# A woven inverse tail, spectra and tables stored as two parts, and pairwise sums, in a one-core hybrid encoder layer

## The chip, the cores and the metric

The kernel runs on one core of one Trainium2 chip. The metric is the device time of one execution in microseconds (us), lower is better. The core has a matrix engine (PE, with its weight loads listed apart as PEld), a vector engine (DVE), a scalar engine (ACT), GpSimd (POOL) and a queue that issues transfers (SP). Each takes its instructions in a fixed order, and all ordinary transfers of this kernel are issued by SP from one queue.

## The reference

One encoder layer on x of 4096 tokens by 1024, all float32. The inputs include the two filter MLPs' weights, convolution weights and gate matrices, which are left out here.

```python
xn = rmsnorm(x, norm_g)
proj = xn @ w_in                                 # 1024 -> 4608 columns: six groups of 768
v, x0, x1 = dwconv3(proj[:, 0:2304])             # centred, width 3
u = v * x1
k = two_sided_filter(MLP(positions)) * exp_window        # 2L points, L1-normalised per channel
y_hy = x0 * (irfft(rfft(u, 2L) * rfft(k, 2L))[:L] + hy_skip * u)
xb = dwconv4(proj[:, 3072:3840])
y_lru = scan_forward(xb) + scan_backward(xb)     # gated linear recurrences, 12 heads of 64
y = concat(rmsnorm(y_hy) * silu(gate_hy), rmsnorm(y_lru) * silu(gate_lru)) @ w_out
out = rmsnorm(x + y, final_g)
```

## The kernel before

Every matmul of float32 operands is done as three products. An operand is split into a high part, rounded to the matmul type, and a low part, the rest; high by high, high by low and low by high are summed in PSUM. A helper `split` (L499 to L501) makes the two parts: ACT copies, DVE subtracts. `mm3` (L503 to L506) issues the three products for 768 columns as six matmuls of 384 columns, so all transforms of the convolution share L506.

- **phase_x** (L238 to L261) normalises x, 128 tokens at a time: two half-row squares on ACT with a running sum, a square root, a reciprocal, transposes, and it stores each chunk of 512 tokens as two parts in DRAM (`xs`) for the later passes.
- **inproj** (L296 on) is the projection. It has 36 column blocks by 8 chunks, each a "unit" of 24 matmuls of 128x512 on L311 to L313. Blocks go in five passes of 7 or 8; `load_w` (L273 to L279) brings a block's weights in two halves of 256 KB (L277), which DVE splits (L278, L279). The first pass is made while x is normalised.
- **phase_filter** makes the filter and its first transform, 64 slices `j`: result `kw` (one part, 384 KB) goes to the table `efd`. **phase_u** does the same for u with 32 slices of 768 KB to `eud`; DVE casts and subtracts on L635 and L636.
- **phase_mid** (L653 on) goes over 64 frequencies `k`. It loads `ef` and `eu` (384 KB each, L658), splits them (ACT L659, POOL L660), loads a table (128 KB, L665) and splits it on POOL (L669, L670), makes two transforms of 6 matmuls, multiplies them as complex numbers (ACT L683 to L685, DVE L689 to L692), splits the product into `rs`, transforms back with 6 matmuls, and stores 384 KB to `eyd` (L703).
- **phase_iy** is the last transform: 32 units, each loading 768 KB of `eyd` (L736, three buffers by `NE`), splitting it (ACT L738, DVE L739), 12 matmuls of 384 columns (L745), one copy (L749) and two stores to `ytd` (L751).
- **phase_out** takes 256 tokens at a time in 32 tasks, one for each branch `r` (0 the convolution, 1 the recurrence). `prepare` loads S (the gate) and y, multiplies and splits them into `A`, squares y (L791), sums the six blocks on DVE with one strided reduction (L796), splits the sum on POOL (L798, L799) and sums over partitions on PE (L803), which gives the scale `rr`. `project` does 72 matmuls (L817 to L819) and adds to the output with `rr` (L821); `finish` normalises and stores. Tasks of r=1 run `LEAD` = 3 chunks ahead of those of r=0, which need `ytd`.

The order is set in two steps. `weave` merges the streams of the phases as they are written, by weights per step; then a scheduler with its own model of the engines fixes one order for each engine and for SP. The recurrence runs beside projection units, then the chain of phase_u, phase_mid and phase_iy beside the remaining 112 units, and phase_out comes last, alone. On SP at most 8 transfers are outstanding: each waits for the one eight before it. A store waits at the queue's head until its data are there, and everything behind it waits too.

Of the kernel before, what the change touches and what calls it, by code (L numbers as in the profile page):

```python
# [25 lines left out]
TC = 512  # L26
NE = 3
NO = 8
# [22 lines left out]
def shape_constants():  # L51
# [54 lines left out]
    fi = fi.reshape(2, 64, 64).transpose(1, 0, 2).reshape(128, 64)  # L106
    return dict(c_zf=zf, c_tn=tn, c_absd=absd.astype(f), c_fa=fa.astype(f), c_tabs=np.stack([tb, ib], 2).astype(f), c_fi=fi.astype(f))


@with_exitstack  # L110
def tile_hymba_block(ctx: ExitStack, tc: tile.TileContext, a: dict, out: bass.AP, dbg=None):
# [119 lines left out]
    def phase_x():  # L231
        tiles = []
        with tc.tile_pool(name="xp", bufs=1, side="right") as xp:
            for n in range(NCH):
# [3 lines left out]
                for q in range(4):  # L238
                    t0 = n * TC + q * P
                    nc.sync.dma_start(xt[q], a["x"][0, t0:t0 + P, :])  # L240
                    for h in range(2):
                        sq = xpool.tile([P, 4, P], F32, name="s4", bufs=3).rearrange("p k e -> p (k e)")
                        nc.scalar.activation(sq, xt[q][:, h * TC:(h + 1) * TC], AF.Square, accum_out=ss[:, h, q:q + 1])
                    qs = slice(q, q + 1) if n == 0 else slice(0, 4)
                    if n == 0 or q == 3:
                        nc.vector.tensor_tensor(rt[:, qs], ss[:, 0, qs], ss[:, 1, qs], ALU.add)
                        nc.scalar.activation(rt[:, qs], rt[:, qs], AF.Sqrt, bias=epsb, scale=1.0 / D)
# [270 lines left out]
    def phase_filter():  # L518
        with ExitStack() as st:
# [51 lines left out]
            hv3 = [t.rearrange("k (p j) -> k p j", j=64) for t in hid]  # L571
            ev = ef_d.rearrange("k r j c -> (k r) j c")
            def first_dft(j, kw, kr):
# [6 lines left out]
            for j in list(range(1, 64)) + [0]:  # L580
                lh = lhs[j % 2]
                for i in range(2):
# [11 lines left out]
                if pend is not None:  # L594
                    first_dft(*pend)
                kw = fw.tile([P, C], F32, name="kw", bufs=3)
                nc.vector.tensor_tensor(cv2(kw), hv(ps), cv2(win), ALU.mult)
# [16 lines left out]
                split(kr, kw)  # L614
                pend = (j, kw, kr)
                yield 0.8
# [3 lines left out]
    def phase_u():  # L620
        JB = 2
        with tc.tile_pool(name="uu", bufs=1) as up:
# [5 lines left out]
            nc.vector.tensor_tensor(fu[:, 1], f0, fu[:, 0].bitcast(F32), ALU.subtract)  # L628
            ev = eu_d.rearrange("k r j c -> (k r) j c")
            uv = ut_d.rearrange("(p j) c -> p j c", j=64)  # L630
            for g in range(64 // JB):
                ui = up.tile([64, JB, C], F32, name="uin", bufs=3)
                nc.sync.dma_start(ui, uv[:, g * JB:(g + 1) * JB, :])
                t = up.tile([P, JB, C], F32R, name="ut", bufs=2)
                nc.vector.tensor_copy(t[0:64], ui)  # L635
                nc.vector.tensor_tensor(t[64:], ui, t[0:64].bitcast(F32), ALU.subtract)  # L636
                stg = up.tile([P, JB, C], F32, name="ustg", bufs=3)
                for j in range(JB):
                    ps = aux_ps()
                    for h in range(2):  # L640
                        for w in range(2):
                            nc.tensor.matmul(ps[:, h, :NH], lhsT=fu[:, w], rhs=t[:, j, h * NH:(h + 1) * NH],  # L642
                                             start=w == 0, stop=w == 1)
                    nc.scalar.activation(cv2(stg[:, j]), hv(ps), AF.Copy)
                nc.sync.dma_start(ev[:, g * JB:(g + 1) * JB, :], stg)
                yield WU
# [6 lines left out]
    def phase_mid():  # L653
        with tc.tile_pool(name="mid", bufs=1) as mp:
            def load(src, s, name, eng):
                t = mp.tile([P, 2, C], F32R, name=name, bufs=3)
                raw = t[:, 1].bitcast(F32)
                nc.sync.dma_start(raw, src[s].rearrange("r j c -> (r j) c"))  # L658
                nc.scalar.activation(t[:, 0], raw, AF.Copy)  # L659
                eng.tensor_tensor(t[:, 1], raw, t[:, 0].bitcast(F32), ALU.subtract)  # L660
                return t

            def tabs(k):
                raw = mp.tile([P, 2, P], F32, name="traw", bufs=2)
                nc.sync.dma_start(raw, a["c_tabs"][:, k])  # L665
                r = []
                for i, (nm, nb) in enumerate((("tb", 2), ("ib", 2))):
                    t = mp.tile([P, 2, P], F32R, name=nm, bufs=nb)
                    nc.gpsimd.tensor_scalar(t[:, 0], raw[:, i], 1.0, 0.0, op0=ALU.mult, op1=ALU.add)  # L669
                    nc.gpsimd.tensor_tensor(t[:, 1], raw[:, i], t[:, 0].bitcast(F32), ALU.subtract)  # L670
                    r.append(t)
                return r

# [32 lines left out]
            for k in range(64):  # L706
                ef, eu = load(ef_d, k, "ef", nc.gpsimd), load(eu_d, k, "eu", nc.gpsimd)
                terms = []
# [45 lines left out]

    def phase_out():
        T = 256
        NM = L // T
        with tc.tile_pool(name="oa", bufs=1) as oa, tc.tile_pool(name="ob", bufs=1, side="right") as ob:
            identr = ob.tile([P, P], F32R, name="identr")
# [6 lines left out]
            def prepare(m, r):  # L766
# [13 lines left out]
                if r == 0:  # L780
                    for q in range(2):
                        yt = ob.tile([P, C], F32R, name="yt", bufs=2)
                        nc.sync.dma_start(yt.bitcast(F32), yt_d[m * T + q * P:m * T + (q + 1) * P, :])
# [14 lines left out]
                nc.gpsimd.tensor_copy(sr[:, 0], sy)  # L798
                nc.gpsimd.tensor_tensor(sr[:, 1], sy, sr[:, 0].bitcast(F32), ALU.subtract)  # L799
                pss = mm_ps()[:, 0:4].rearrange("p (q w) -> p q w", w=2)  # L800
# [5 lines left out]
                nc.vector.reciprocal(rr, rr)  # L806
                return A, rr

            def project(m, r, A, rr):
                for q in range(2):  # L810
                    ps = aux_ps()
                    for h in range(2):
                        sl = slice(h * 512, (h + 1) * 512)
                        for b in range(CB):
# [3 lines left out]
                            nc.tensor.matmul(ps[:, h], lhsT=ht, rhs=w[:, 1, sl], start=False, stop=False)  # L818
                            nc.tensor.matmul(ps[:, h], lhsT=lt, rhs=w[:, 0, sl], start=False, stop=b == CB - 1)  # L819
                    o = os_[m][q]  # L820
                    nc.vector.scalar_tensor_tensor(o, ps.rearrange("p h c -> p (h c)"), rr[:, q:q + 1], o,  # L821
                                                   op0=ALU.mult, op1=ALU.add)

            def finish(m):
                for q, o in enumerate(os_.pop(m)):
                    sq = ob.tile([P, D], F32, name="osq", bufs=2)
                    fs = ob.tile([P, 1], F32, name="fs", bufs=4)
# [10 lines left out]
            for i, t in enumerate(tasks):  # L838
                nxt = prepare(*tasks[i + 1]) if i + 1 < len(tasks) else None
                if i == 0:  # L840
                    for j in range(CB):
                        load_wo(j, main.tile([P, 2, KT, P], F32R, name="w", bufs=NW) if len(wos) < NW
                                else ob.tile([P, 2, KT, P], F32R, name=f"w{j}"),
                                lambda: oa.tile([P, TC], F32, name="ostg", bufs=2))
                    gfin.append(ob.tile([P, D], F32, name="gfin"))
                    nc.sync.dma_start(gfin[0], a["final_g"].partition_broadcast(P))
# [36 lines left out]
    phase_out()  # L883
    psctx.close()
# [29 lines left out]
```

## Time and profile before

| | us |
|---|---|
| median of 3 runs | 2957.67 (2956.57 to 2961.78) |
| the profiled execution | 2955.19 |
| its span in the trace | 2953.4 |
| PE busy in the span | 2848.1 (96%) |
| DVE, ACT, POOL busy | 1997.9, 1697.9, 705.9 |
| bytes moved | 699 MB, mean 237 GB/s |

The page's times are of the one profiled execution; the 1.8 us outside its span are its start and end. A busy PE is not a PE at its peak pace: matmuls overlap, so the time lost is read from gaps and from distances between starts. The span in 40 slices shows the PE at nine tenths or more nearly throughout, with dips in the first slice and around 2350 us, and the granted clock below full in two slices there.

### The profile page before, as it was taken

How to read it: one execution, taken by the hardware profiler on the slowest of the kernel's cores; microseconds unless marked ns; L12 is line 12 of the kernel's file. 1: busy time of each engine (PE TensorE's matmuls, PEld its weight loads, DVE VectorE, ACT ScalarE, POOL GpSimd, SP SyncE). 2: the span in 40 equal slices, each digit the busy share in tenths (PEclk: the TensorE clock that was granted, in tenths of full speed). 3: DMA queues.
4: the chain of work that ended last, by engine and by line, in shares of the span. 5: the costliest groups of instructions: out<-in, count | busy, mean ns of one | idle time of the engine just before them, and what ended most of it. 6: DMA issues, size and time to landing. Idle time of an engine off the chain costs nothing.

```text
span 2953.4 us, 37821 instructions
## 1 busy us (share of the span) xinstructions
PE 2848.1 (96%) x13211; PEld 2386.2 (81%) x13211; DVE 1997.9 (68%) x2144; ACT 1697.9 (57%) x2534; POOL 705.9 (24%) x910
## 2 busy tenths in 40 slices
PE   7999999999999999999999998999999799999998
PEld 6778888888887787877888887888888678888886
DVE  6998879664768856787664788666643366666665
ACT  4678887767787676764445675666645432222222
POOL 0013323210101201111004776766710010000001
PEclk9999999999999999999999999999999889999999
DMA  7566657437879877787997677666679865455542
GB/s 273 210 219 235 232 215 250 177 136 244 292 273 309 291 277 249 258 310 225 357 342 277 227 239 259 230 231 238 235 276 309 280 211 164 164 182 169 176 154 75
DMA packets 338238, 699.33 MB, mean 237 GB/s; under 512 B 33821, under 2 KB 156145, under 8 KB 337791
## 3 DMA queue, kind: packets, MB, share of 16 engines
q1 hardware_dynamic: 337918, 696.85, 67.9%
q8 instruction: 105, 1.72, 0.2%
q14 instruction: 87, 0.70, 0.1%
q0 software_dynamic: 128, 0.05, 0.0%
HBM read 445.13 MB, written 251.66 MB: 236 GB/s over the span
## 4 chain that ended last, share of the span: by engine, by line
PE 65%; DVE 13%; DMA 9%; issue 5%; ACT 5%; POOL 3%; SPq 1%; DVEq 0%; ACTq 0%; POOLq 0%
PE mm L311 12%; PE mm L312 12%; PE mm L313 12%; PE aux L506 8%; PE aux L819 4%; PE aux L817 4%; PE aux L818 4%; PE aux L443 3%; DVE cv L343 2%; PE aux L745 2%; DMA eu<-eud 2%; DMA x<-xs 2%; DVE sy L796 2%; PE aux L642 2%; DVE bb L470 1%
## 5 line engine op out<-in xcount | busy, mean ns | idle before, releaser
L311 PE MATMUL mm<-x,w 128*128 128x512 f32 x2304 | 909.3, 396 | 12.6 <-ACT cv L341 5.6
L312 PE MATMUL mm<-x,w 128*128 128x512 f32 x2304 | 907.6, 394 | 0.1
L313 PE MATMUL mm<-x,w 128*128 128x512 f32 x2304 | 905.2, 394 | 0.0
L311 PEld LDWEIGHTS mm<-x,w 128*128 128x128 f32 x2304 | 435.2, 189 | 105.3 <-DMA x<-xs 9.3
L313 PEld LDWEIGHTS mm<-x,w 128*128 128x128 f32 x2304 | 434.7, 189 | 84.4 <-issue 0.5
L312 PEld LDWEIGHTS mm<-x,w 128*128 128x128 f32 x2304 | 434.9, 189 | 84.1 <-issue 1.4
L817 PE MATMUL aux<-w,A 128*128 128x512 f32 x768 | 305.7, 398 | 19.0 <-DMA y<-yld 19.0
L343 DVE SCALAR_TENSOR_TENSOR cv<-raw,cols,cv 128x512 f32<-128x512 f32 (+2 forms) x336 | 260.7, 780 | 85.7 <-ACT cv L341 81.2
L819 PE MATMUL aux<-w,A 128*128 128x512 f32 x768 | 305.2, 401 | 0.0
L818 PE MATMUL aux<-w,A 128*128 128x512 f32 x768 | 304.4, 396 | 0.0
L798 POOL CAST sr<-sy 128x256 fp32r<-128x256 f32 x32 | 39.2, 1226 | 703.4 <-DVE sy L796 498.2
L660 POOL TENSOR_TENSOR ef<-ef 128x768 fp32r<-128x768 f32 x64 | 129.1, 2017 | 239.3 <-DMA eu<-eud 195.2
L817 PEld LDWEIGHTS aux<-w,A 128*128 128x128 f32 x768 | 146.1, 190 | 49.6 <-ACT A L793 19.3
L818 PEld LDWEIGHTS aux<-w,A 128*128 128x128 f32 x768 | 146.0, 190 | 32.0
L819 PEld LDWEIGHTS aux<-w,A 128*128 128x128 f32 x768 | 145.9, 190 | 30.9
L501 DVE TENSOR_TENSOR rs<-r,rs 128x768 fp32r<-128x768 f32 x65 | 94.1, 1447 | 108.3 <-ACT rs L500 108.3
L791 ACT ACTIVATE y<-y 128x1536 f32<-128x1536 f32 x32 | 47.7, 1490 | 202.8 <-DVE S L790 180.9
L333 ACT ACTIVATE raw<-mm 128x512 f32<-128x512 f32 x192 | 113.3, 590 | 86.0 <-PE mm L313 85.6
L443 PE MATMUL aux<-hl,wg 128*128 128x512 f32 x576 | 147.8, 392 | 5.4 <-ACT bb L445 5.2
L477 POOL TENSOR_TENSOR xb<-xb,bb 128x1024 f32<-128x1024 f32 x24 | 65.2, 2719 | 292.5 <-DVE bb L470 203.6
L660 POOL TENSOR_TENSOR eu<-eu 128x768 fp32r<-128x768 f32 x64 | 124.3, 1943 | 39.0 <-ACT eu L659 38.9
L443 PEld LDWEIGHTS aux<-hl,wg 128*128 128x128 f32 x576 | 107.3, 188 | 29.3 <-ACT bb L445 6.8
(201 smaller groups left out, 5023.6 us busy)
## 6 DMA issues: line engine op xcount, KB each, us to landing
x<-xs SPq DMA_DIRECT2D x256, 512.0 KB
hl<-hld SPq DMA_DIRECT2D x96, 512.0 KB
xs<-x SPq DMA_DIRECT2D x64, 512.0 KB
efd<-kw SPq DMA_DIRECT2D x64, 384.0 KB
sd<-cv SPq DMA_DIRECT2D x96, 256.0 KB
xb<-xbd SPq DMA_DIRECT2D x48, 512.0 KB
eud<-ustg SPq DMA_DIRECT2D x32, 768.0 KB
ef<-efd SPq DMA_DIRECT2D x64, 384.0 KB
```

The costliest lines, as they stand in the source:

```text
L311: nc.tensor.matmul(ps, lhsT=w[:, 0, kt, :], rhs=x[kt][:, 0], start=kt == 0, stop=False)
L312: nc.tensor.matmul(ps, lhsT=w[:, 0, kt, :], rhs=x[kt][:, 1], start=False, stop=False)
L313: nc.tensor.matmul(ps, lhsT=w[:, 1, kt, :], rhs=x[kt][:, 0], start=False, stop=kt == KT - 1)
L333: nc.scalar.activation(R[:, K - 1:K - 1 + TC], ps, AF.Copy)
L343: nc.vector.scalar_tensor_tensor(y[:, :N], R[:, k:k + N], w[k], y[:, :N], op0=ALU.mult, op1=ALU.add)
L443: nc.tensor.matmul(ps[:, h], lhsT=wg[:, u, gi, :], rhs=hl[h][:, v], start=k == 0, stop=k == 2)
L501: nc.vector.tensor_tensor(dst[:, 1], src, dst[:, 0].bitcast(F32), ALU.subtract)
L506: nc.tensor.matmul(ps[:, h, :NH], lhsT=lhs[:, x], rhs=rhs[:, y, h * NH:(h + 1) * NH], start=first and i == 0, stop=last and i == 2)
L660: eng.tensor_tensor(t[:, 1], raw, t[:, 0].bitcast(F32), ALU.subtract)
L817: nc.tensor.matmul(ps[:, h], lhsT=ht, rhs=w[:, 0, sl], start=b == 0, stop=False)
L818: nc.tensor.matmul(ps[:, h], lhsT=ht, rhs=w[:, 1, sl], start=False, stop=False)
L819: nc.tensor.matmul(ps[:, h], lhsT=lt, rhs=w[:, 0, sl], start=False, stop=b == CB - 1)
```

## The change

- Two-part storage. `efd` and `eud` hold a high and a low part, written by phase_filter (DVE subtracts the low part on a new line) and phase_u, so phase_mid loads 768 KB instead of 384 KB for each of `ef` and `eu` and splits neither. The transform table comes from the host as two parts; 65 transfers of 256 KB copy it from the input to a DRAM tensor `tabd` (written in phase_filter's loop), and phase_mid loads 256 KB per `k` from there. POOL does nothing in phase_mid any more.
- Buffers. `e` of phase_iy goes from 3 to 2, the staging of phase_u and of the filter (`kw`) from 3 to 2; phase_mid's table has 3.
- phase_u's cast moves from DVE to ACT.
- Weaving. 24 of phase_iy's 32 units are merged with phase_u, phase_mid and the projection; the last 8 (`TAIL`) come between phase_out's first tasks, which are of r=1. Pools of phase_out that need room come later (`late`).
- Sums. The strided reduction L796 becomes three elementwise adds; POOL's split becomes an ACT copy and a DVE subtract; the partition sums (`token_scale`) are made within `project`, after its first 36 matmuls.
- Squares. For the first chunk each whole row of 1024 is squared with a running sum once, by ACT for two of its tiles and by DVE for the other two.

```diff
-NE = 3
+NE = 2
+TAIL = 8
...
-    ef_d = dram.tile([64, 2, 64, C], F32, name="efd")
-    eu_d = dram.tile([64, 2, 64, C], F32, name="eud")
+    ef_d = dram.tile([64, 2, 64, 2, C], F32, name="efd")
+    eu_d = dram.tile([64, 2, 64, 2, C], F32, name="eud")
+    tab_d = dram.tile([P, 65, 2, 2, P], F32, name="tabd")
...
+                    if n == 0:
+                        sq = aux_ps().rearrange("p h c -> p (h c)")
+                        if q % 2:
+                            nc.vector.tensor_tensor_reduce(out=sq, in0=xt[q], in1=xt[q], scale=1.0, scalar=0.0, op0=ALU.mult,
+                                                           op1=ALU.add, accum_out=ss[:, 0, q:q + 1])
+                        else:
+                            nc.scalar.activation(sq, xt[q], AF.Square, accum_out=ss[:, 0, q:q + 1])
...
-                nc.scalar.activation(cv2(kw), hv(ps), AF.Copy)
-                nc.sync.dma_start(ev[:, j, :], kw)
+                nc.scalar.activation(cv2(kr[:, 0]), hv(ps), AF.Copy)
+                nc.vector.tensor_tensor(cv2(kr[:, 1]), hv(ps), cv2(kr[:, 0].bitcast(F32)), ALU.subtract)
+                nc.sync.dma_start(ev[:, j], kr.bitcast(F32))
...
             for j in list(range(1, 64)) + [0]:
+                nc.sync.dma_start(tab_d[:, j], a["c_tabs"][:, j])
...
-                raw = t[:, 1].bitcast(F32)
-                nc.sync.dma_start(raw, src[s].rearrange("r j c -> (r j) c"))
-                nc.scalar.activation(t[:, 0], raw, AF.Copy)
-                eng.tensor_tensor(t[:, 1], raw, t[:, 0].bitcast(F32), ALU.subtract)
+                nc.sync.dma_start(t.bitcast(F32), src[s].rearrange("r j w c -> (r j) w c"))
...
+                t = mp.tile([P, 2, 2, P], F32R, name="tab", bufs=3)
+                nc.sync.dma_start(t.bitcast(F32), tab_d[:, k])
+                return t[:, 0], t[:, 1]
...
-                sy = ob.tile([P, T], F32, name="sy", bufs=2)
-                nc.vector.tensor_reduce(sy, y.rearrange("p b t -> p t b"), axis=mybir.AxisListType.X, op=ALU.add)
+                nc.vector.tensor_tensor(y[:, 0:3], y[:, 0:3], y[:, 3:6], ALU.add)
+                nc.vector.tensor_tensor(y[:, 0], y[:, 0], y[:, 1], ALU.add)
+                sy = y[:, 0]
+                nc.vector.tensor_tensor(sy, sy, y[:, 2], ALU.add)
...
-                nxt = prepare(*tasks[i + 1]) if i + 1 < len(tasks) else None
+                nxt = prepare(*tasks[i + 1]) if i + 1 < len(tasks) and i + 1 != LEAD else None
+                if i < LEAD - 1:
+                    for _ in itertools.islice(tail, TAIL // (LEAD - 1)):
+                        pass
...
-    weave((proj, 144 - X2), (itertools.chain(phase_u(), phase_mid(), phase_iy()), (32 * WU + 129 * WM + 32 * WI) * S3))
+    last = phase_iy()
+    weave((proj, 144 - X2), (itertools.chain(phase_u(), phase_mid(), itertools.islice(last, 32 - TAIL)),
+                             (32 * WU + 129 * WM + (32 - TAIL) * WI) * S3))
```

The three places below show what the scheduler made of it. First, SP's queue at the start, where the weights of the first pass are loaded (`s` from `in_w_in`), before:

```order
12 L277 DMA s_339<-in_w_in_dram 128x4x128
13 L277 DMA s_343<-in_w_in_dram 128x4x128
14 L261 DMA xs_0_60<-x 128x1024
15 L261 DMA xs_1_61<-x 128x1024
16 L277 DMA s_348<-in_w_in_dram 128x4x128
17 L261 DMA xs_2_62<-x 128x1024
18 L277 DMA s_352<-in_w_in_dram 128x4x128
```

And the same place after, with the table copies (`tabd` from `in_c_tabs`, x8 being eight in a row):

```order
14 L596 DMA tabd<-in_c_tabs_dram 128x512 x2
15 L291 DMA s_337<-in_w_in_dram 128x4x128
16 L596 DMA tabd<-in_c_tabs_dram 128x512 x8
17 L291 DMA s_341<-in_w_in_dram 128x4x128
18 L596 DMA tabd<-in_c_tabs_dram 128x512 x3
19 L291 DMA s_346<-in_w_in_dram 128x4x128
20 L596 DMA tabd<-in_c_tabs_dram 128x512 x6
21 L291 DMA s_350<-in_w_in_dram 128x4x128
22 L596 DMA tabd<-in_c_tabs_dram 128x512 x3
```

All 65 copies stand in SP's rows 14 to 57, between the weight loads of the first pass, although they are written in the filter's loop; four of the sixteen weight halves stand behind all of them.

Second, PE's order where phase_mid's last inverse transform (`aux` from `rs`) stands, before; `mm` from `x,w` is a matmul of the projection:

```order
7155 L506 MATMUL aux<-rs,ib 128x384
7156 L313 MATMUL mm<-x,w 128x512
7157 L311 MATMUL mm<-x,w 128x512
7158 L312 MATMUL mm<-x,w 128x512
7159 L313 MATMUL mm<-x,w 128x512
7160 L506 MATMUL aux<-rs,ib 128x384 x5
7161 L311 MATMUL mm<-x,w 128x512
```

And after, where the last projection matmul (row 7534) stands:

```order
7531 L520 MATMUL aux<-rs,tab 128x384 x5
7532 L325 MATMUL mm<-x,w 128x512
7533 L326 MATMUL mm<-x,w 128x512
7534 L327 MATMUL mm<-x,w 128x512
7535 L520 MATMUL aux<-ef,tab 128x384 x6
7536 L520 MATMUL aux<-eu,tab 128x384 x6
7537 L520 MATMUL aux<-rs,tab 128x384 x6
7538 L520 MATMUL aux<-ef,tab 128x384 x6
```

Before, 426 projection matmuls follow the last inverse transform of phase_mid. After, none is left when 22 of its 65 `ef` transforms, 22 of `eu` and 23 of `rs` are still to come: PE has nothing else to do between them.

Third, PE's order where phase_out begins (`aux` from `w,A`), before:

```order
7649 L311 MATMUL mm<-x,w 128x512
7650 L312 MATMUL mm<-x,w 128x512
7651 L313 MATMUL mm<-x,w 128x512
7652 L745 MATMUL aux<-es,fi 128x384 x60
7653 L817 MATMUL aux<-w,A 128x512
7654 L818 MATMUL aux<-w,A 128x512
7655 L817 MATMUL aux<-w,A 128x512
```

And after:

```order
7600 L520 MATMUL aux<-rs,tab 128x384 x17
7601 L821 MATMUL mm<-onesr,sr 128x2 x8
7602 L755 MATMUL aux<-es,fi 128x384 x325
7603 L836 MATMUL aux<-w,A 128x512
7604 L837 MATMUL aux<-w,A 128x512
7605 L838 MATMUL aux<-w,A 128x512
```

Before, 5 units of phase_iy (60 matmuls) stand alone between the projection and phase_out. After, 27 of them (325 matmuls) stand alone, and the other 5 between 91 matmuls of phase_out's first task.

## Rows read from the trace of the kernel before

**Rows 1.** Windows: busy us (instructions) of PE, PEld, DVE, ACT, POOL; clock, DMA share, GB/s.
```profile
0.00:100.00 100.00, 85.23 (x370) 65.32 (x371) 75.46 (x156) 55.61 (x129) 3.06 (x11) 1.00 0.76 269
...
1400.00:1500.00 100.00, 97.13 (x448) 84.53 (x449) 65.11 (x54) 41.60 (x69) 0.00 (x0) 0.97 1.00 352
...
1700.00:1800.00 100.00, 93.24 (x437) 78.37 (x435) 83.59 (x85) 65.66 (x91) 73.66 (x66) 1.00 0.67 227
...
2300.00:2400.00 100.00, 76.59 (x353) 65.19 (x352) 47.95 (x38) 42.09 (x46) 9.38 (x6) 0.88 0.82 272
```

**Rows 2.** Shorter windows, the same columns.
```profile
30.00:40.00 10.00, 9.03 (x40) 7.16 (x39) 6.82 (x12) 4.70 (x12) 0.00 (x0) 1.00 1.03 369
...
60.00:70.00 10.00, 7.88 (x42) 6.20 (x41) 6.42 (x12) 4.38 (x13) 0.00 (x0) 1.00 0.08 32
1000.00:1005.00 5.00, 5.00 (x24) 4.13 (x22) 4.96 (x5) 4.39 (x5) 2.53 (x1) 1.00 1.03 419
...
2350.00:2360.00 10.00, 0.00 (x0) 0.00 (x0) 1.76 (x1) 0.40 (x1) 0.00 (x0) 0.50 1.04 374
```

**Rows 3.** Timeline of SP at the start: start us, us, engine, line.
```profile
51.36 0.38 SPq L277 DMA_DIRECT2D s<-in_w_in_dram  x1
```

**Rows 4.** Timeline of DVE at the start, the same columns.
```profile
54.52 0.43 DVE L278 CAST w<-s 128x512 fp32r<-128x512 f32 x1 [0.33 <-DMA s<-in_w_in_dram]
```

**Rows 5.** DMA issues: queue, count, KB each.
```profile
ef<-efd SPq DMA_DIRECT2D x64, 384.0 KB
...
eyd<-r SPq DMA_DIRECT2D x64, 384.0 KB
e<-eyd SPq DMA_DIRECT2D x32, 768.0 KB
...
s<-in_w_in_dram SPq DMA_DIRECT2D x72, 256.0 KB
...
traw<-in_c_tabs_dram SPq DMA_DIRECT2D x65, 128.0 KB
```

**Rows 6.** Timeline of PE: starts of two matmuls of 512 columns in phase_out.
```profile
2387.15 0.39 PE L818 MATMUL aux<-w,A 128*128 128x512 f32 x1
2387.38 0.39 PE L819 MATMUL aux<-w,A 128*128 128x512 f32 x1
```

**Rows 7.** Groups by shape, 1600 to 2150 us: busy, mean ns of one, idle before.
```profile
L692 DVE SCALAR_TENSOR_TENSOR r<-us,sgn,r 128x768 f32<-128x768 f32 x61 | 92.0, 1508 | 1.9
L501 DVE TENSOR_TENSOR rs<-r,rs 128x768 fp32r<-128x768 f32 x61 | 89.7, 1471 | 104.5 <-ACT rs L500 104.5
L506 PE MATMUL aux<-rs,ib 128*128 128x384 f32 x367 | 86.4, 346 | 20.7 <-DVE rs L501 11.0 <-issue 5.6 <-POOL tb L669 1.9
...
L691 DVE TENSOR_TENSOR r<-aux,ha 128x768 f32<-128x768 f32 x61 | 58.4, 958 | 1.7
```

**Rows 8.** Groups by shape, 300 to 600 us (the filter).
```profile
L501 DVE TENSOR_TENSOR kr<-kw,kr 128x768 fp32r<-128x768 f32 x45 | 42.9, 954 | 0.0
```

**Rows 9.** Groups by shape, 2050 to 2340 us (phase_iy).
```profile
L739 DVE TENSOR_TENSOR es<-e,es 128x1536 fp32r<-128x1536 f32 x32 | 56.3, 1759 | 88.2 <-ACT es L738 81.7 <-DMA x<-xs 6.5
L738 ACT ACTIVATE es<-e 128x1536 fp32r<-128x1536 f32 x32 | 47.4, 1482 | 8.3 <-DMA e<-eyd 5.1 <-DMA fz<-in_c_fi_dram 3.2
```

**Rows 10.** Timeline of PE where phase_out begins.
```profile
2335.07 2.35 PE L745 MATMUL aux<-es,fi 128*128 128x384 f32 x12 [1.35 <-DVE es L739]
2337.81 2.36 PE L745 MATMUL aux<-es,fi 128*128 128x384 f32 x12 [0.39 <-DVE es L739]
2341.32 2.19 PE L745 MATMUL aux<-es,fi 128*128 128x384 f32 x11 [1.15 <-DVE es L739]
2362.51 0.80 PE L817 MATMUL aux<-w,A 128*128 128x512 f32 x1 [19.01 <-DMA y<-yld]
```

**Rows 11.** Waits of PE: engine, line, for what, us in total, times, longest.
```profile
PE mm L803 <- POOL sr L798: 10.1, 16, 2.6
```

**Rows 12.** Groups by shape, 2340 us to the end (phase_out).
```profile
L796 DVE TENSOR_REDUCE sy<-y 128x256 f32<-128x1536 f32 x32 | 92.8, 2936 | 8.1 <-ACT y L791 8.1
```

More of the change, by code (lines that the diff above doesn't have):

```diff
@@ L240, in phase_x @@
                     nc.sync.dma_start(xt[q], a["x"][0, t0:t0 + P, :])
-                    for h in range(2):
+                    if n == 0:
[5 more added lines that the diff above has]
+                            nc.scalar.activation(sq, xt[q], AF.Square, accum_out=ss[:, 0, q:q + 1])
+                    for h in range(2 if n else 0):
                         sq = xpool.tile([P, 4, P], F32, name="s4", bufs=3).rearrange("p k e -> p (k e)")
@@ L706, in phase_mid @@
             for k in range(64):
-                ef, eu = load(ef_d, k, "ef", nc.gpsimd), load(eu_d, k, "eu", nc.gpsimd)
+                ef, eu = load(ef_d, k, "ef"), load(eu_d, k, "eu")
                 terms = []
@@ L752, in phase_iy, with phase_out @@
                 yield WI
-    def phase_out():
+    def phase_out(tail):
         T = 256
         NM = L // T
-        with tc.tile_pool(name="oa", bufs=1) as oa, tc.tile_pool(name="ob", bufs=1, side="right") as ob:
+        with ExitStack() as st:
+            oa = st.enter_context(tc.tile_pool(name="oa", bufs=1, side="right"))
+            ob = st.enter_context(tc.tile_pool(name="ob", bufs=1, side="right"))
+            late = {}
             identr = ob.tile([P, P], F32R, name="identr")
@@ L806, in prepare, with project @@
                 nc.vector.reciprocal(rr, rr)
[L807 to L809 removed]
+                return rr
+            def project(m, r, A, sr):
+                rr = None
                 for q in range(2):
@@ L838, in phase_out @@
             for i, t in enumerate(tasks):
-                nxt = prepare(*tasks[i + 1]) if i + 1 < len(tasks) else None
-                if i == 0:
-                    for j in range(CB):
+                nxt = prepare(*tasks[i + 1]) if i + 1 < len(tasks) and i + 1 != LEAD else None
+                if i < LEAD - 1:
+                    for _ in itertools.islice(tail, TAIL // (LEAD - 1)):
+                        pass
+                if i == LEAD - 1:
+                    for _ in tail:
+                        pass
+                    late["pool"] = st.enter_context(tc.tile_pool(name="oc", bufs=1))
+                    nxt = prepare(*tasks[i + 1])
+                if i in (0, LEAD - 1):
+                    for j in (range(2), range(2, CB))[i > 0]:
                         load_wo(j, main.tile([P, 2, KT, P], F32R, name="w", bufs=NW) if len(wos) < NW
-                                else ob.tile([P, 2, KT, P], F32R, name=f"w{j}"),
+                                else late["pool"].tile([P, 2, KT, P], F32R, name=f"w{j}"),
                                 lambda: oa.tile([P, TC], F32, name="ostg", bufs=2))
-                    gfin.append(ob.tile([P, D], F32, name="gfin"))
+                if i == LEAD - 1:
+                    gfin.append(late["pool"].tile([P, D], F32, name="gfin"))
                     nc.sync.dma_start(gfin[0], a["final_g"].partition_broadcast(P))
@@ L880, in tile_hymba_block @@
     pcfg.update(pool=psctx.enter_context(tc.tile_pool(name="psb", bufs=1, space=PSUM)), aux=3, hi=1)
-    weave((proj, 144 - X2), (itertools.chain(phase_u(), phase_mid(), phase_iy()), (32 * WU + 129 * WM + 32 * WI) * S3))
+    last = phase_iy()
+    weave((proj, 144 - X2), (itertools.chain(phase_u(), phase_mid(), itertools.islice(last, 32 - TAIL)),
+                             (32 * WU + 129 * WM + (32 - TAIL) * WI) * S3))
     right.close()
-    phase_out()
+    phase_out(last)
     psctx.close()
```

55 lines of the change are left out of this document (29 added, 26 removed).

## The prediction

> **What bounds the kernel now.** I read the windows of 100 us first. PE, with 92 to 100 us busy of nearly every 100, sets the time: what counts is the waits of PE that a change removes or adds. Three stretches stand out: the start (85.23 busy), the spectra (93.24 in 1700:1800), and the passage to the output, where 76.59 us are busy and the clock is 0.88 [rows 1]. Second, the transfers. They reach 369 GB/s when the queue is full for 10 us, 374 beside an idle PE, 419 for 5 us, and 352 over a whole 100 us with the DMA share at 1.00 [rows 1, 2]. So 352 to 369 GB/s is what a long stretch can have here, 419 the outermost bound. Third, PE's own pace. Two matmuls of 512 columns start 0.23 us apart [rows 6], which makes 0.172 for 384 columns; a run of 12 of these takes 2.36 us and one of 11 2.19, so one more costs 0.17 [rows 10]. One `k` of the spectra, 18 such matmuls, is 3.1 us of PE, a unit of phase_iy 2.06.
>
> The change takes nothing from PE's work, so its gains are waits, and it adds bytes: the two-part tables double `efd` and `eud` on the way out (49 MB more) and `ef`, `eu` on the way in (50 MB more), and the copies of the tables read 17 MB more and write them, with 8.5 MB more loaded: 697 MB become 823 MB. Where this hurts depends on where PE has other work in the meantime, which the order shows.
>
> **The change part by part.** Nine terms, added to the profiled execution (2955.2 us).
>
> *Start.* All weight loads of the first pass go through SP's queue, where the last of them is issued at 51.36 us and its half is taken up by DVE at 54.52 [rows 3, 4]. Up to there I add 17.1 MB from the order of before. After, the 65 copies of 256 KB, 17.0 MB, stand between these loads, and 33.6 MB are issued up to the last. At 369 GB/s [rows 2] that is 91 us, some 94 with the first 3 us, 40 later than now. PE needs each half in turn and has nothing else written there, so it waits. It gets back some 4 us: in 60:70 the transfers rest at 32 GB/s and PE loses 2 us there for chunk 1's preparation [rows 2], which would be finished. **+36**. At 419 GB/s it would be 33.6 / 0.419 = 80 us, some +23. On the other side no row of before has a transfer that both starts and ends in DRAM: if such a copy has half the rate, 17.0 MB take 92 us in place of 46, and the term is +82.
>
> *Filter and u.* 64 subtractions of 0.954 us [rows 8] are added to DVE in the filter, and the staging has one buffer less. DVE has room beside the woven projection units. In phase_u, SP issues 102 MB between its first load and its last store, and PE has 265 us of work there; at 352 GB/s the bytes need 290. Before it was 59 MB beside 154 us, which need 168, and PE lost only 3 of 100 us there [rows 1]: the excess of 14 was largely absorbed by what was already loaded. Taking 25 less 14 for that: **+10** for both, between 0 and 25.
>
> *Woven part of the spectra.* The row of the inverse transform shows 20.7 us of PE idle, most of it behind the DVE split of `rs` and some behind POOL [rows 7]. POOL's work on both spectra and the table goes, and DVE's L692 and L501 take 1508 and 1471 ns here [rows 7] where the same subtraction takes 954 in the filter with little on POOL [rows 8]. The Trainium skill ("SBUF — State Buffer", section "SBUF: two separate sides") has DVE and GpSimd share a port pair that is held as an exclusive lock by whichever starts first; the two durations agree with it. The product chain is thus some 1.1 us shorter per `k`. I take two thirds of the 20.7, **-14**; between -25 and, if 127 MB in 449 us of PE work (284 GB/s) come in the wrong moments, +20.
>
> *Spectra alone.* After the last projection matmul, 22 `k` follow with nothing between. Each moves 768 + 768 + 256 + 384 KB, 2.23 MB, in place of 1.31 by the sizes now [rows 5]. With 8 MB of gates, y and output weights in the same stretch of the queue and 6 MB that are loaded ahead, some 51 MB remain: at 369 GB/s 138 us, against 22 x 3.1 = 68 us of PE. **+70**. At 419 it is +54, at 352 +77. The engines alone leave less: DVE's three products of 0.96 us (L691 stands for them [rows 7]), the sum and the split at 0.95 each make 4.8 us per `k`, +37, which is the bound if the transfers were no limit.
>
> *Passage to phase_iy.* Each of its units reads rows from all 64 `k`, so the last store of `eyd` must land first. Before, 426 projection matmuls cover this. After, copy (0.8), store (2.7), load of 768 KB (2.1 at rate and 2 until it lands), ACT 1.48 and DVE 1.76 [rows 9] stand in a row, with only eight tiny matmuls for PE: **+10**, between 5 and 12.
>
> *phase_iy alone.* 27 units stand alone where there were 5. Units alone came 2.74 and 3.51 us apart with three `e` buffers [rows 10]. With two, a buffer is held for the load (about 4.1) and its ACT and DVE steps (3.24), 7.4 us for two units: 3.7 each in place of 2.06. 27 x 1.64 = **+44**. At the spacing of before it is 27 x 1.06 = +28; at 4.2 us it is +58.
>
> *Passage to phase_out.* PE waited 19.01 us for y [rows 10], with the clock at 0.50 in 2350:2360 [rows 2], and the lower clock lasted until the transfers had come; 2300:2400 lacks 23.4 us of PE in all [rows 1]. After, the first tasks are prepared before phase_iy and its last five units stand among the first task's matmuls. **-28**, between -20 and -33.
>
> *phase_out.* PE waits 10.1 us for POOL's part of the row sums [rows 11]. Three adds of a half, a sixth and a sixth of the elements replace the reduction of 2.94 us [rows 12], and the partition sums come 36 matmuls later, so most of it goes: **-8**, between -10 and 0.
>
> *First squares.* Two half rows on ACT become one row on either engine, while PE waits for weights anyway: **-1**, at most -3.
>
> Sum: 36 + 10 - 14 + 70 + 10 + 44 - 28 - 8 - 1 = **+119**, so 3074 us for a profiled execution, and **3077** as a median, since the median of the runs stands 2.5 above the profiled one.
>
> **The rivals.** *A: copies at half rate.* Everything else as above, but a copy uses the memory twice, +82 in place of +36 at the start: 3077 + 46 = 3123. For it: each byte is read and written. Against it: single stretches already move 419 GB/s [rows 2]. The Trainium skill ("DMA: Bandwidth & Descriptors", section "Where 436 GB/s comes from") gives a core about 358 GB/s of its memory; the 419 of this trace is above it, so the trace does not agree for short stretches. By the page's figure a copy would have half, 179 GB/s, and the copies would take 95 us, an estimate.
>
> *B: the transfers keep their burst rate.* At 419 GB/s throughout, with the better end of the others: 23 + 0 - 25 + 54 + 5 + 28 - 28 - 8 - 1 = +48, 3006. For it: one window of 5 us. Against it: every window of 10 us or more is at 386 or below, as far as I have looked.
>
> *C: the relieved engines win.* The order of the tail was fixed by a model of the transfers; if the tables are in place well ahead, the copies fit into the gaps of the first 70 us, and PE's stops in the spectra (20.7 and some 10 of small ones), the passage (28) and phase_out (8) all go while the 22 `k` alone run at DVE's 4.8 us (+37) and phase_iy at the old spacing with the wait gone: -31 - 28 - 8 + 37 - 10 = -40, 2917. The place is the stretch without projection matmuls. It decides for faster where the starved stretches together cost less than the 77 or so that goes. For it: the stops of before are real. Against it: 2.23 MB in 4.8 us is 465 GB/s, more than any row shows.
>
> **How the numbers follow.** The forecast's case has 0.73, A 0.10, B 0.10, C 0.07. The forecast's own range, with its terms' ends partly cancelling, is 3040 to 3115. The range that holds the time 8 times in 10 takes in A's value with its own spread and most of B: 3000 to 3150. A measurement of this kernel tells about 0.2% (6 us) from no change. Faster by more than that: 0.07, from C; within it: 0.03, from the near ends of B and C; slower: 0.90.
>
> **What would show it.** Start: `tabd` copies between the weight loads in SP's timeline, the last weight half near 95 us, PE idle in 30:90 behind DMA. Spectra: a stretch of some 140 us with no `mm` matmul in which the DMA share is near 1.00, PE below 60% busy and `ef`, `eu` loads as what ends its waits; if DVE ends them, the floor of 4.8 us was the limit. phase_iy: units 3.5 to 4 us apart. The passage: no wait of 19 us for y, but one near 10 for the first `e`. phase_out: no wait for a POOL step. The forecast is wrong if the copies land early, if the stretch without projection work runs near PE's pace, or if the clock falls for long in the thinly filled stretches, which I have not put in as a term of its own.

## The result, and the profile after

The changed kernel takes 3151.6 us (3151.25 to 3152.1) against 2957.1: a ratio of 1.0669 [1.0655, 1.0683], some 195 us slower. The forecast was 3077 us, range 3000 to 3150, and the time lies just above that range. The direction was right, and so were most of the places; the size was not.

The windows of 100 us of the changed kernel, with the columns of [rows 1], show where the time stands:

```profile
0.00:100.00 100.00, 43.19 (x163) 31.93 (x164) 37.34 (x76) 19.38 (x41) 3.03 (x11) 0.83 0.97 342
...
2000.00:2100.00 100.00, 100.00 (x480) 87.57 (x479) 49.61 (x53) 47.58 (x62) 0.00 (x0) 1.00 0.91 345
...
2200.00:2300.00 100.00, 74.05 (x319) 65.94 (x318) 73.07 (x79) 60.65 (x77) 0.00 (x0) 0.82 0.97 350
2300.00:2400.00 100.00, 65.90 (x238) 58.42 (x237) 61.95 (x66) 53.25 (x67) 0.00 (x0) 0.74 0.78 273
2400.00:2500.00 100.00, 58.74 (x210) 50.66 (x208) 41.38 (x40) 45.27 (x46) 0.00 (x0) 0.73 0.76 261
```

The first window has less than half the matmuls of before. The spectra beside the projection (2000:2100) leave PE no gap at all, where 1700:1800 of before had 93.24 [rows 1]. Then, with no projection left, PE has 238 and 210 matmuls in 100 us instead of some 470, at a granted clock of 0.74 and 0.73.

To compare stretches whose matmuls stand in another order, I take the time lost: the time that has passed at an instruction less the PE work up to it, counted from all starts of the trace at the paces of [rows 6] and [rows 10]. It holds stops of PE and also what PE runs below its full pace. Differences of that, in us:

| stretch | lost before | lost after | difference | forecast |
|---|---|---|---|---|
| start to the filter's first transform | 34 | 85 | +51 | +36 -1 |
| filter | 9 | 15 | +6 | (with u) +10 |
| recurrence, to u's first transform | 40 | 61 | +21 | none |
| u | 5 | 7 | +1 | see above |
| spectra beside projection | 49 | 7 | -42 | -14 |
| 22 k of the spectra alone | 0 | 109 | +109 | +70 |
| passage to phase_iy | 0 | 10 | +10 | +10 |
| phase_iy alone | 6 | 77 | +71 | +44 |
| passage to the output's first transposes | 25 | 3 | -22 | -28 |
| output | 41 | 33 | -8 | -8 |

The start, in DVE's and PE's timelines after (the second DVE row is the last half of the first pass and answers to [rows 4], 54.52 there):

```profile
94.51 0.43 DVE L292 CAST w<-s 128x512 fp32r<-128x512 f32 x1 [11.85 <-DMA s<-in_w_in_dram]
...
101.00 0.42 DVE L292 CAST w<-s 128x512 fp32r<-128x512 f32 x1
```

```profile
96.48 0.79 PE L325 MATMUL mm<-x,w 128*128 128x512 f32 x1 [24.15 <-ACT cv L355]
```

The last half comes 46 us later, where 40 were forecast, and PE stops once for 24 us. ACT, named as releaser, was long done: it is the wait for several semaphores of which the weight was the last.

The same start has a second wait, of 11 us, that the forecast did not have. PE's timeline after, then DVE's:

```profile
20.86 0.48 PE L269 MATMUL xt<-ident,xt 128*128 128x128 f32 x1 [11.19 <-DVE xt L264]
```

```profile
16.64 0.43 DVE L292 CAST w<-s 128x512 fp32r<-128x512 f32 x1 [4.68 <-DMA s<-in_w_in_dram]
16.99 1.23 DVE L250 CUSTOM_DVE_ANT_0 aux<-xt 128x1024 f32<-128x1024 f32 x1
...
20.07 0.73 DVE L264 TENSOR_SCALAR xt<-xt,rt 128x1024 f32<-128x1024 f32 x1
```

The first chunk's square on DVE takes 1.23 us, but it stands behind a weight cast that waits for its load until 16.64. The first transposes, at 8.0 us before, start at 20.9.

The stretch without projection, in the chain of waits after (start, us, what):

```profile
2301.26 5.82 DMA tab<-tabd
...
2307.21 5.22 PE aux L520 x18
...
2312.46 6.07 DMA tab<-tabd
...
2318.66 4.50 PE aux L520 x17
```

A table of 256 KB takes some 6 us to land. It stands behind 1.5 MB of `ef` and `eu`, and 1.8 MB at the 307 GB/s of this stretch would be 6 us, an estimate. Its issue waits for a buffer that PE frees. In this chain load and use take turns. The end of the stretch has almost no transfers left:

```profile
2400.00:2420.00 20.00, 10.51 (x33) 8.14 (x31) 9.93 (x11) 7.96 (x11) 0.00 (x0) 0.67 0.24 92
```

phase_iy alone, in PE's timeline after (answering to [rows 10]):

```profile
2489.30 0.44 PE L755 MATMUL aux<-es,fi 128*128 128x384 f32 x1 [1.15 <-ACT es L748]
2491.10 3.35 PE L755 MATMUL aux<-es,fi 128*128 128x384 f32 x12 [1.35 <-DVE es L749]
2494.93 2.46 PE L755 MATMUL aux<-es,fi 128*128 128x384 f32 x11 [0.48 <-DVE es L749]
2499.03 0.44 PE L755 MATMUL aux<-es,fi 128*128 128x384 f32 x1 [1.64 <-ACT es L748]
```

From the first of its matmuls at 2426.3 to the output's at 2559.7 it is 133 us for 27 units, 4.94 each where 3.7 was forecast.

### The profile page after: what moved, and what is told of

It reads as the page before. It is cut to its first block, busy times and chain, and to the rows that moved or that the text cites. A ratio compares the mean times of both kernels' runs of the same rounds, so it can differ in the third digit from the quotient of the medians.

```text
span 3149.6 us, 37278 instructions
## 1 busy us (share of the span) xinstructions
PE 2914.8 (93%) x13211; PEld 2438.1 (77%) x13211; DVE 1982.0 (63%) x2336; ACT 1669.2 (53%) x2463; POOL 220.0 (7%) x458
## 4 chain that ended last, share of the span: by engine, by line
PE 72%; DMA 11%; DVE 9%; ACT 4%; issue 4%; SPq 1%; ACTq 0%; DVEq 0%
PE mm L325 13%; PE mm L326 13%; PE mm L327 13%; PE aux L520 10%; PE aux L836 6%; PE aux L838 5%; PE aux L837 5%; PE aux L457 3%; DMA e<-eyd 2%; DMA tab<-tabd 2%; DVE cv L357 2%; PE aux L660 1%; DVE bb L484 1%; DMA tabd<-in_c_tabs_dram 1%; DMA s<-in_w_in_dram 1%
## 5 line engine op out<-in xcount | busy, mean ns | idle before, releaser
L699 DVE TENSOR_TENSOR us<-aux,hb 64x768 f32<-64x768 f32 x65 | 62.3, 959 | 201.9 <-ACT hb L695 172.0
L755 PE MATMUL aux<-es,fi 128*128 128x384 f32 x384 | 99.2, 417 | 51.1 <-ACT es L748 26.3
L755 PEld LDWEIGHTS aux<-es,fi 128*128 128x128 f32 x384 | 86.7, 241 | 63.0 <-DVE es L749 31.5
L418 ACT ACTIVATE cv<-mm 128x512 f32<-128x512 f32 x96 | 57.2, 597 | 137.0 <-PE mm L327 124.4
L520 PE MATMUL aux<-rs,tab 128*128 128x384 f32 x390 | 98.0, 373 | 32.3 <-ACT rs L514 17.0
```

The source lines that it names most:

```text
L520: nc.tensor.matmul(ps[:, h, :NH], lhsT=lhs[:, x], rhs=rhs[:, y, h * NH:(h + 1) * NH], start=first and i == 0, stop=last and i == 2)
L699: nc.vector.tensor_tensor(cv2(us)[0:64], pu[64:], cv2(hb)[64:], ALU.mult)
L755: nc.tensor.matmul(ps[:, h, :NH], lhsT=fi[:, fp, i], rhs=es[:, ep, i, h * NH:(h + 1) * NH], start=m == 0, stop=m == 5)
```

## The experiments

Ratios are against the kernel before on the same chip; the changed kernel's is 1.0669. A hundredth is about 29.5 us, and the intervals allow each ratio some 3 to 7 us either way.

**The squares.** The edit of e1 takes `if n == 0:` with its two whole-row squares out, so that `for h in range(2):` makes half rows for every chunk.

> The changed kernel with the first chunk's squares as before (half rows, on ACT only). In the changed kernel the first transposes start at 20.9 us instead of 8.0, because DVE's squares stand in its queue behind a weight cast (L292) that waits for its load until 16.6. Theory A (this wait is paid): first transposes back near 9 us and some 9 us less in all, 3142. Theory B (the 65 copies hold up the weights, whose last half is there near 97 us whatever x does): the transposes come early, PE waits longer for weights, and the time stays within 3 us of 3151.6.

Ratio 1.0657 [1.0633, 1.0682], not told apart from the changed kernel. The transposes start at 7.9 us, the last half is taken up at 104 instead of 101, and at the filter's first transform 82 us are lost instead of 85. The ratio alone can't rule out the 9 us of theory A, which lie at the edge of its interval; the 3 us of the trace speak for theory B, here. But with the copies out of the way the start lost 32 us up to the last parameter transpose with the whole-row squares (e2), 20 with half rows (e6). The squares cost 12 us, hidden behind a larger wait.

**The table copies.**

```diff
-                nc.sync.dma_start(tab_d[:, j], a["c_tabs"][:, j])
-                if j == 0:
-                    nc.sync.dma_start(tab_d[:, 64], a["c_tabs"][:, 64])
...
+                for jj in ([j, 64] if j == 0 else [j]):
+                    nc.sync.dma_start(tab_d[0:1, jj, 0, 0], kr[0:1, 0, 0:P].bitcast(F32))
+                    nc.sync.dma_start(tab_d[:, jj], a["c_tabs"][:, jj])
                 pend = (j, kr)
```

> The changed kernel, but each table copy is made to follow the filter step in whose loop it is written (a small store from that step's result to the same place of tabd goes ahead of it), so that no copy stands between the first weight loads. Theory A (copies ahead of the weights cost the start): the last weight half is there near 55 to 60 us and the time falls by 35 to 45, to 3107 to 3117. Theory B (the bytes have to be moved anyway and the filter, with a DMA share of 0.64 to 0.76, has no room): the start gets better but the filter's stores wait, 3135 to 3151.

1.0524 [1.0502, 1.0547]: 43 us less, theory A. The last weight half of the first pass is there at 45 us, earlier than expected and than in the kernel before (54.52). That row in DVE's timeline of e2, and the windows:

```profile
45.05 0.43 DVE L292 CAST w<-s 128x512 fp32r<-128x512 f32 x1 [0.43 <-DMA s<-in_w_in_dram]
```

```profile
0.00:100.00 100.00, 74.33 (x325) 56.62 (x326) 71.74 (x144) 46.16 (x98) 3.01 (x11) 1.00 0.72 259
...
300.00:400.00 100.00, 100.00 (x506) 86.81 (x505) 85.58 (x115) 75.12 (x140) 23.76 (x66) 1.00 0.83 303
```

The filter takes the 17 MB without a gap in PE in this window, and up to its last transform it loses no more than in the changed kernel. The copies are as dear as the order makes them.

**PE's work and clock in the stretch alone.**

```diff
                 ps = aux_ps()
+                if s >= 40:
+                    for h in range(2):
+                        for i in range(WARM):                     # 6
+                            nc.tensor.matmul(ps[:, h, :NH], lhsT=terms[0][0][:, 0], rhs=terms[0][1][:, 0, h * NH:(h + 1) * NH],
+                                             start=i == 0, stop=i == WARM - 1)
```

> The changed kernel with 12 extra matmuls of 384 columns ahead of each inverse transform from k = 40 on, into the same bank, overwritten by the real ones: 24 x 12 x 0.173 = 50 us more PE work in the stretch without projection. Theory A (transfers set that stretch): time unchanged within 10 us, granted clock up. Theory B (the loop from PE's release of a buffer to the next load sets it, and PE's half clock lengthens the loop): the clock goes from 0.74 to above 0.9 there and the real matmuls halve in time, 10 to 30 us less, 3120 to 3141. Theory C (the extra work stands in the loop and the clock does not matter): 25 to 50 us more, 3177 to 3200.

1.0684 [1.0666, 1.0702]: unchanged, the time of theory A. The window 2240 to 2400 of the changed kernel, then of e3:

```profile
2240.00:2400.00 160.00, 99.94 (x360) 88.92 (x360) 107.54 (x115) 89.72 (x110) 0.00 (x0) 0.72 0.87 307
```

```profile
2240.00:2400.00 160.00, 121.75 (x590) 112.80 (x589) 104.86 (x112) 87.44 (x107) 0.00 (x0) 0.90 0.85 307
```

590 matmuls instead of 360, clock 0.90 instead of 0.72, and the same 307 GB/s and 20 `k` in 160 us. PE is busy 6.1 us per `k` instead of 5.0, and the `k` come no slower: PE's waits for a table fall from 31 to 14 us instead. So PE's busy time by itself does not set this stretch, and neither does DVE's, which is busy for two thirds of it. But the run changed two things that pull opposite ways, more matmuls and a higher clock (the median matmul on `ef` went from 0.52 to 0.33 us). Theories B and C together would leave the time unchanged too, so what the low clock alone cost stays open.

**The order tied to the projection.**

```diff
-S3 = 1.6
+S3 = 0.8
...
+                nc.tensor.matmul(mm_ps()[:, :NH], lhsT=terms[0][0][:, 0], rhs=terms[0][1][:, 0, :NH], start=True, stop=True)
                 o = mp.tile([P, C], F32, name="r", bufs=3)
```

> The changed kernel with one extra matmul per k that uses the projection's PSUM buffers (64 x 0.17 = 11 us more PE work) and S3 = 0.8: the buffers' rotation ties the order of the spectra to that of the projection units as they are written, so 1013 projection matmuls stand after the last inverse transform instead of none, and 14 units of phase_iy alone instead of 27 less those under way. All bytes are the same. Theory A (the 22 k and 27 units cost what they do because nothing covers their waits): the stretch from u's first to phase_out loses some 90 us instead of 210, which is what 343 MB at 360 GB/s need beyond 868 us of PE work: 3010 to 3060. Theory B (the waits come with the bytes and move into the woven part): 3120 to 3160.

1.1039 [1.1018, 1.1059]: 109 us slower than the changed kernel, 11 of them the added matmuls; outside both. Two windows of e4:

```profile
1550.00:1700.00 150.00, 83.35 (x280) 69.49 (x278) 89.53 (x78) 74.37 (x83) 0.00 (x0) 0.65 0.93 345
2350.00:2550.00 200.00, 200.00 (x910) 169.05 (x909) 20.40 (x14) 44.26 (x56) 0.00 (x0) 1.00 0.60 210
```

u's doubled stores now stood nearly alone in the first, starved at a DMA share of 0.93, and the projection that was left ran in the second, where the transfers had little to do. The order of the changed kernel was the better one for its bytes; mine crowded them.

**The spectra's second part.** e5 takes the lines on `efd`, `eud`, `first_dft`, `ustg` and phase_mid's `load` back to those of before, with three staging buffers for u and the filter.

> The changed kernel with efd and eud stored as one part again and split in phase_mid by ACT and POOL, as before; table copies, squares, weaving and sums stay as changed. 100 MB fewer bytes. The order then has 316 projection matmuls after the last inverse transform and 9 units of phase_iy alone before phase_out, instead of none and 27. Theory A (the doubled bytes make both the order without cover and its price): the start still loses some 50, the stretch of the 22 k (109), its passage (10) and most of phase_iy's 77 go, and the woven part pays about 30 for POOL's splits again: 2995 to 3030. Theory B (the weaving and the two e buffers, not the spectra, cost the tail): 3080 to 3150.

1.0128 [1.0114, 1.0142], 2991 us: 160 of the 195 us go, theory A, at the lower end of its range or a little under it. The edit takes the bytes and, with them, the order without cover: the run shows what both cost together. The recurrence loses 41 us again instead of 61. Here, as before, some 17 fewer projection units stand beside the filter than in the changed kernel, whose filter has twice the bytes to store, and the recurrence has them to cover its own waits. About 10 of the 21 us are one place: in the changed kernel PE waits 7.5 and 2.3 us right behind the filter's last transform, with no projection matmul to run; before and in e5 it does not.

**An even tie.** e2's copies, half-row squares, four table buffers, e4's line, and:

```diff
-S3 = 1.6
-WU = 0.5
-WM = 0.27
-WI = 2.2
+S3 = 1.0
+WU = 1.0
+WM = 0.42
+WI = 0.8
```

> Late copies as in e2, half-row squares, four table buffers, and the pinned order of e4 with weights by bytes (WU 1.0, WM 0.42, WI 0.8, S3 1.0), so that spectra and projection end together: 459 projection matmuls after the last inverse transform, 4 units of phase_iy alone. The bytes are those of the changed kernel. Theory A (in e4 the bytes were only crowded into the first half, and the limit is the 343 MB from u to phase_iy at some 360 GB/s): the stretch loses 80 to 110 in place of 207 in e2, 3000 to 3035. Theory B (any tie of the spectra to the projection makes PE wait in order for them): 3100 or more.

1.0371 [1.0355, 1.0387]: between the two; 45 us under e2, of which 12 are the squares. From u to the output it needs 1009 us at 330 GB/s with a DMA share of 0.90, in place of 1048 at 324 in the changed kernel and 959 at 269 before. Covering the waits helps by some 30, in which the fourth table buffer has its part (e10); 50 us over the kernel before are left, 11 of them the added matmuls. That the rest is the bytes is argued: no run has them with another order still.

**The parts that do not move bytes.** e8 makes the sums' edit of the diff in the kernel before; e7 adds the woven tail with its pools, two `e` buffers and u's cast on ACT.

> The kernel before with only the sums changed: three elementwise adds for the strided reduction, ACT and DVE in place of POOL for the split, and the partition sums after the task's first 36 matmuls. Theory A (PE's 10.1 us behind POOL's step go, DVE loses nothing): 6 to 10 us less, ratio 0.9966 to 0.998. Theory B (the passage's wait for y is the only thing there that counts, and the partition sums in the middle of a task stop PE elsewhere): ratio 0.999 to 1.002.

> The kernel before with the woven tail (TAIL 8, two e buffers, late pools), the pairwise sums with the later partition sums, and u's cast on ACT; no table copies, one-part spectra and tables, half-row squares. Its order has 433 projection matmuls after the last inverse transform and 4 units of phase_iy alone ahead of phase_out, 4 beside its first 85 matmuls. Theory A (these parts do what the trace of after shows of them: passage -22, phase_out -8): 25 to 32 us under the kernel before, ratio 0.989 to 0.992. Theory B (the passage's wait for y only moves to the first loads of phase_iy or to the weights): ratio 0.997 to 1.003.

e8: 0.9969 [0.9959, 0.9979], theory A. e7: 0.9990 [0.9981, 0.9998], theory B: what e7 adds to the sums costs about 6 us. PE's timeline at its passage:

```profile
2344.40 0.79 PE L827 MATMUL aux<-w,A 128*128 128x512 f32 x1 [7.77 <-ACT A L797]
2378.16 0.69 PE L746 MATMUL aux<-es,fi 128*128 128x384 f32 x1 [9.61 <-ACT es L739]
```

One wait of 19 us became two of 8 and 10: the loads of both are on one queue, and each side waits for its share. In the changed kernel the passage lost only 3 us, and there the loads for the output ran in the starved stretch ahead of it. So the 22 us seem to be bought there; no run tests it. e8's PE waits confirm the sums: the wait behind POOL's step [rows 11] is gone, and the passage now waits for the output weights.

```profile
PE aux L823 <- DMA ostg<-in_w_out_dram: 22.9, 1, 22.9
```

**Buffers.**

```diff
-NE = 2
+NE = 3
...
-                o = ip.tile([P, C], F32, name="yo", bufs=3)
+                o = ip.tile([P, C], F32, name="yo", bufs=2)
```

> The changed kernel with three e buffers in phase_iy (and two instead of three staging buffers yo behind it, for room). PE's order is the changed kernel's, 27 units alone. Theory A (the loop of two buffers, load 5 to 6 us then ACT and DVE, sets the 4.9 us per unit): 27 units at 3.2 to 3.9, 27 to 45 us less, 3107 to 3125. Theory B (the transfers, at 250 to 330 GB/s with the DMA share at 0.8 to 0.9, set it): at most 10 us less, 3140 to 3152.

1.0576 [1.0561, 1.0590], 27 us less: theory A at its edge, 4.02 us per unit. The window 2480 to 2530 of the changed kernel and of e9:

```profile
2480.00:2530.00 50.00, 30.94 (x129) 26.01 (x129) 19.62 (x12) 24.25 (x22) 0.00 (x0) 0.89 0.81 248
```

```profile
2480.00:2530.00 50.00, 37.03 (x169) 31.70 (x170) 24.38 (x14) 30.70 (x28) 0.00 (x0) 0.93 0.93 332
```

The third buffer fills the queue, from 248 to 332 GB/s in this window. That the bytes then hold the unit at 4 us is argued from the DMA share of 0.93.

> The changed kernel with four table buffers in phase_mid instead of three; 19 k alone after the last projection matmul instead of 22. In the changed kernel the chain of that stretch alternates between a table load (some 6 us from issue to landing, behind 1.5 MB of ef and eu) and PE's matmuls. Theory A (that loop sets the 8.0 us per k): 6.6 us per k, what its 2.45 MB need at 369 GB/s, and with 19 of them 179 us become some 130: 3100 to 3115. Theory B (bytes and the three ef and eu buffers set it): 7.5 to 8 us per k, at most 25 less by the 3 k that are covered, 3127 to 3150.

Its edit is `bufs=4` for `tab`. 1.0607 [1.0591, 1.0623], 18 us less: theory B, by its range and by its pace of some 7.5 us per `k`, where A had 6.6. In its 2240 to 2360:

```profile
2240.00:2360.00 120.00, 74.92 (x285) 64.96 (x284) 87.93 (x93) 70.67 (x87) 0.00 (x0) 0.80 0.96 343
```

In the same 120 us the changed kernel moved 374, 316 and 286 GB/s per 40 us, 325 in the mean, at a DMA share of 0.92. PE's waits for a table, 31 us in 2240:2400 of the changed kernel, are gone in e10, and ACT and DVE end its waits instead. So the three buffers did keep the queue from being full, but by little: 10 to 15 of the 18 us are the 2 or 3 `k` that are now covered, at some 5 us lost by each, and the rest is pace. e10's 7.5 us per `k` moves 2.57 MB, output loads included, at a share of 0.96.

**A version that beats both.** The sums of e8 and e2's copies of a two-part table, in the kernel before:

> The kernel before with the sums of e8 and with the table of phase_mid stored as two parts, copied within the filter as in e2; spectra one part, no woven tail, three e buffers. POOL keeps the splits of ef and eu but not the table's four operations per k. The order has 316 projection matmuls after the last inverse transform and 14 units of phase_iy alone. Theory A (POOL's table work is what slows the woven spectra, as e5's 20 us lost there against 49 before suggest, and the longer stretch of phase_iy alone costs less than that): 10 to 25 us under e8, ratio 0.988 to 0.9935. Theory B (what the spectra gain phase_iy loses, since transfers of the same bytes set the sum): ratio 0.995 to 1.000.

0.9972 [0.9961, 0.9984], 2942 us, not told apart from e8: theory B. The spectra beside the projection lose 22 us instead of 49, and phase_iy, with 14 units alone, loses 28 instead of 6. Of theory A's reason only a part holds: DVE's two steps still take 1555 and 1217 ns there, beside POOL's splits of `ef` and `eu`, and yet most of the 49 us are gone. Both e8 and e11 beat the kernel before by 0.3%.

## Why the prediction was right in direction and too small

The forecast was +119 and the time rose by 195. In the order of the table, the terms missed by +16 at the start, +18 from the filter to u, -28 in the woven spectra, +39 in the spectra alone and +27 in phase_iy alone; the rest missed little. The -28 was luck, which hid a part of the rest: without it the forecast would have been off by some 100.

- **Start: right for the copies.** The last half came at 101, forecast as 94, and e2 gets 43 us back. The squares' term was wrong: not -1 but 12 us, hidden in the changed kernel (e1) and bare without the copies (e2 against e6). I had priced the instruction and not looked at what stands ahead of it on DVE.
- **Filter and u: a place missed.** u cost 1 and the filter 6, but the recurrence between them lost 21 more, which was in no term. The longer filter took projection units that had covered it, and e5 gives them back.
- **Spectra beside the projection: the right sign, three times the size.** -42. The two steps on DVE take 1019 and 959 ns here (1508 and 1471 in [rows 7]) with no POOL work beside them:

```profile
L702 DVE SCALAR_TENSOR_TENSOR r<-us,sgn,r 128x768 f32<-128x768 f32 x39 | 39.7, 1019 | 1.4
...
L515 DVE TENSOR_TENSOR rs<-r,rs 128x768 fp32r<-128x768 f32 x39 | 37.4, 959 | 46.3 <-ACT rs L514 46.2
```

  Nearly all of the 49 us went. I had taken two thirds of the 20.7 us that one row showed as idle, where by the measure of the table 49 were lost. The faster DVE steps, which I gave as the reason, explain the smaller part: in e5 and e11 they are still slow (1419 and 1257 ns, 1555 and 1217 ns) and only 20 and 22 us are lost. The larger part went there with the table's operations on POOL, or with the order, which puts more projection beside the spectra in both of them and in the changed kernel; no run tells these two apart.
- **Spectra alone, the step that failed most: +70 forecast, +109 measured.** The term took 51 MB "at 369 GB/s", 138 us. The bytes were about right (49 MB in 160 us), the rate was not: it was 307, with a DMA share of 0.87 and not near 1.00, and that is some 27 of the 39 us. The other 12 or so are the end, for which the sum had no term: the last 16 us, when the engines finish the last `k` with almost nothing left to load. What ended PE's waits in the stretch was not `ef` or `eu`, as forecast, but the table (33 us in all) and the product's steps on ACT and DVE (30); some 40 us more of the 109 are its matmuls at the lower clock, which it may have had time for. A fourth table buffer gives 18 back, most of it by the `k` that it covers (e10). What holds the rest of the rate down stays open.
- **phase_iy alone: the right loop with a load that is too short, +44 against +71.** Two buffers made 4.94 us and not 3.7, since the loads in the chain of waits took 5.3 to 7.1 us where I had 4.1; e9 gives 27 back.
- **Passages and output: right**, +10, -22, -8, but e7 shows that weaving alone does not give the -22: there one wait became two.
- The low clock was left out of the sum without a price. It came, 0.72 in 2240:2400; e3, which raised it together with PE's work, saw no change, and what it cost alone stays open.

The rivals: A (copies at half rate) is out: the weights would have come 46 us later still. B's burst rate was seen nowhere for long. C was right that the stops in the spectra, at the passage and in the output would shrink; that was 72 us, against 270 that were added elsewhere.

## What to carry to other kernels

Trading an engine's split for a second part in memory pays only where the transfers have room: here 42 of the 49 us that the woven spectra lost went, and 190 were added in the stretches where nothing else was left to run. Price a stretch that is alone by its buffers first (bytes per buffer over the loop of load, landing and release) and by the full rate only if that loop leaves room. And look for where a scheduler puts a transfer without operands to wait for: here it went to the front, ahead of what the start needs.

## What the runs showed of the hardware

Copies from DRAM to DRAM did not run at half rate. The trace counts a copy's bytes once: the page of the changed kernel has 826 MB of transfers, while the memory was read and written for 840 MB together, and before the two figures are 699 and 697. In 80:90 of the changed kernel nearly all transfers under way are copies (15 of them are issued from 76.4 to 86.9), in 60:70 about half, and half of the 369 GB/s of [rows 2] would be 185:

```profile
60.00:70.00 10.00, 3.05 (x7) 2.43 (x8) 1.12 (x2) 0.00 (x0) 0.00 (x0) 0.59 1.05 394
...
80.00:90.00 10.00, 0.00 (x0) 0.00 (x0) 1.12 (x2) 0.00 (x0) 0.00 (x0) 0.50 0.99 335
```

And at a DMA share of 0.81, phase_iy alone moved 248 GB/s (2480:2530), at 0.93 332 (the same window of e9): per share the rate is not the same, an estimated 306 and 357 at a full share.

DVE's split of `rs` is slow only while POOL works: in 1600:2150 of the kernel before, 12 of the 61 splits had no POOL instruction beside them and took 959 ns, the other 49 took 1596 ns in the mean. In the changed kernel, with POOL idle there, it took 959 again.
